# A routed mixture-of-experts start rewritten: token rows by ScalarE and GpSimd, nine weight pieces split ahead of the gather

## The chip, the cores and the metric

The kernel runs on one core of a Trainium2 chip. The time is that of one execution in microseconds (us) on the device; lower is better. The core's engines are TensorE (PE, matmuls), VectorE (DVE), ScalarE (ACT), GpSimd (POOL) and SyncE (SP, which here only issues DMAs). Each engine works through its own instructions in order and waits on semaphores for the others.

## What is computed

Two transformer layers on 512 tokens of 1024 columns, then a state-space and pooling block. Layer 0 has dilated attention, layer 1 attention with forgetting; each is followed by a mixture of 16 experts, and only that part is touched here. Cut to it:

```python
def hierarchical_moe(h, wg_r, bg_r, we_r, be_r, w_gate, w_up, w_down):
    t = h.reshape(-1, d)                                  # 512 tokens
    g_prob = softmax(t @ wg_r + bg_r)                     # 4 groups of experts
    g_onehot = one_hot(argmax(g_prob)); g_w = max(g_prob)
    e_sel = einsum('nge,ng->ne', (t @ we_r + be_r).reshape(-1, 4, 4), g_onehot)
    top_v, top_i = top_k(e_sel, 2)                        # two experts of four
    gates = ...                                           # softmax(top_v) * g_w, zero elsewhere
    hid = silu(einsum('nd,edf->nef', t, w_gate)) * einsum('nd,edf->nef', t, w_up)
    y = einsum('nef,efd->nd', hid * gates[..., None], w_down)

hf = rmsnorm(x, norm_ffn[i]) * (1 + sc_f) + sh_f
x = x + g_f * hierarchical_moe(hf, ...)
```

## The kernel before

**Routing.** `moe_route` goes over four tiles of 128 tokens (t = 0 to 3), right behind the mixer's out-projection. For each it scales the rows, transposes them for PE (L850), multiplies by the router weights (L853), computes the inverse norm `tn_r`, forms the logits `lg` (L1205), and `route_tile` (L874 to L891) picks group and experts with short DVE instructions; `route_rank` (L899, L900) counts each token's place in its expert's list. L1209 forms the normed and shifted row `hn` in one DVE instruction of 128x1024, which writes the columns in another order (k major), so that a later transpose meets contiguous columns; SP writes it to `hd` in HBM (L1210).

**Lists and gathers.** In `moe`, `listed(e)` compares ranks with places (`oh`, L948), multiplies by the token numbers on PE (L952), writes the list `tidx` (L953, DVE) and has POOL gather up to 96 rows of `hd` into `xg` (L966). Three `xg` buffers are cleared by POOL beforehand (L1241). `route_gates` (L919 to L941) computes the gates with DVE and two exponentials on ACT.

**Overflow.** If an expert has over 96 tokens, a branch (`tc.If`, L1084) does the rest. Here it has none; still every engine reads the flag, branches, and passes a skip block in which it waits for its own instructions and, on SP and POOL, for the DMAs of its queues. Work that is behind the branch on one engine and waits for another engine's work behind the branch waits for that engine to have passed it.

**Weights.** An expert has six pieces of 0.5 MB: c = 0 to 3 hold gate and up, c = 4 and 5 down. `expert_loads` has SP issue them in order into raw buffers: `est` (7 of them, `DL['nes']`), `esp` (2, for c = 5), and four `x` buffers. The first nine steps of it (`n0` = 8, and one each for the later tiles) are issued in the routing. Matmuls are done in fp32r with the operand split in a high and a low half, three products for one: `split_weights` has ACT write the high half (L316) and DVE the low half (L317) into one of nine `ehl` buffers, used in turn, and the raw buffer is then free for the next load. The first expert is taken plain, in fp32 and without a split: transposed rows in `xTf` (L1021), matmuls on the raw pieces. Piece c = 5 is plain for every expert.

**Order.** PE's instructions are in the order of the code (`manual_schedule`); those of the other engines are placed by a scheduler that interleaves what is independent. `load(n)` stands for n steps of: split a piece, issue the next load.

**Experts.** `step(e)` runs gate and up of expert e (L154), between them the transposes of the next expert's rows (L1019 for the plain form, L487 for the split one), then the hidden part and the down product of the expert before, and `listed(e + 3)`.

## Time and profile before

| | us |
|---|---|
| runs | 1825.73, 1826.6, 1831.0 |
| median | 1826.6 |
| the profiled execution, its own time | 1824.57 |
| its span (first to last instruction) | 1822.6 |
| PE busy in the span | 1624.6 (89%) |
| DVE, ACT, POOL busy | 1285.6, 919.7, 123.9 |
| mixture of layer 0, from the first gather to the last issue of an expert piece | 734 to 904 |
| the same of layer 1 | 1279 to 1448 |

A row of the timeline gives the start, the duration, the engine, the line, the operation, what it writes and reads, and in brackets how long the engine stood idle ahead of it and what ended that. "DVEq L1084" stands for the sequencer of DVE at the branch, SPq for an issue by SP. In the table of stretches PEclk is the granted clock of PE as a share of the full 2.4 GHz, and DMA is the mean busy share of the 16 DMA engines.

### The profile page before, as it was taken

The numbers are of one execution on the slowest core, as the hardware profiler recorded it, in microseconds if no ns is written. First come the engines' busy times: TensorE is split into PE (matmuls) and PEld (weight loads), VectorE is DVE, ScalarE is ACT, GpSimd is POOL, SyncE is SP. The second block draws the span as 40 slices with busy tenths as digits, with TensorE's granted clock in tenths as the row PEclk, the third lists the DMA queues.
The fourth block names the chain that finished last, engine by engine and source line by source line (L and its number), as shares of the span: only waits on it lengthen the run. The fifth ranks groups of instructions, "written<-read, shape, count | busy, mean of one in ns | idle before, by whom it ended". The sixth has DMA issues, their size and how long they took to land. (4 is left out here: it accounts for less than half of the span.)

```text
span 1822.6 us, 29089 instructions
## 1 busy us (share of the span) xinstructions
PE 1624.6 (89%) x10222; PEld 1381.7 (76%) x10223; DVE 1285.6 (71%) x3181; ACT 919.7 (50%) x1975; POOL 123.9 (7%) x101
## 2 busy tenths in 40 slices
PE   5979999999999998699859999898689959999998
PEld 3778999989989987456548798887455647788886
DVE  6758677677776656688755768757688746998564
ACT  4536455565555652566533655642556534353443
POOL 1000000000000000133210000000132210000000
PEclk9999999999999998799989999999799979999999
DMA  8786546466564235799872231226799854233331
GB/s 291 225 282 206 170 146 195 148 180 187 153 182 120 84 100 193 235 306 323 271 185 71 71 89 51 76 82 208 232 315 314 266 168 116 78 106 99 111 117 72
DMA packets 263995, 310.90 MB, mean 171 GB/s; under 512 B 33887, under 2 KB 177867, under 8 KB 263836
## 3 DMA queue, kind: packets, MB, share of 16 engines
q1 hardware_dynamic: 255708, 291.89, 51.1%
q0 software_dynamic: 8128, 17.02, 4.2%
q8 instruction: 84, 1.38, 0.3%
q14 instruction: 75, 0.61, 0.1%
HBM read 287.88 MB, written 38.90 MB: 179 GB/s over the span
## 5 line engine op out<-in xcount | busy, mean ns | idle before, releaser
L154 PE MATMUL mm<-whi,hThi 128*128 128x384 f32 (+2 forms) x1128 | 401.7, 356 | 5.4 <-DVE vlo L420 2.5
L154 PE MATMUL mm<-whi,hTlo 128*128 128x384 f32 (+2 forms) x1128 | 382.4, 339 | 0.8 <-DVE hTlo L741 0.6
L154 PE MATMUL mm<-wlo,hThi 128*128 128x384 f32 (+2 forms) x1128 | 381.1, 338 | 0.0
L317 DVE TENSOR_TENSOR wlo<-wst,whi 128x768 fp32r<-128x768 f32 (+2 forms) x200 | 199.6, 1009 | 69.4 <-ACT whi L316 66.9
L154 PEld LDWEIGHTS mm<-whi,hThi 128*128 128x128 f32 x1128 | 214.2, 190 | 15.0 <-DVE vlo L420 3.1
L316 ACT ACTIVATE whi<-wst 128x768 fp32r<-128x768 f32 (+2 forms) x200 | 176.1, 890 | 92.7 <-PE mm L154 54.3
L317 DVE TENSOR_TENSOR ehl<-est,ehl 128x1024 fp32r<-128x1024 f32 x144 | 175.7, 1220 | 61.5 <-ACT ehl L316 47.2
L154 PEld LDWEIGHTS mm<-whi,hTlo 128*128 128x128 f32 x1128 | 213.9, 190 | 4.4 <-DVE hTlo L741 1.8
L154 PEld LDWEIGHTS mm<-wlo,hThi 128*128 128x128 f32 x1128 | 214.8, 190 | 1.9 <-issue 0.6
L316 ACT ACTIVATE ehl<-est 128x1024 fp32r<-128x1024 f32 x144 | 152.1, 1058 | 110.5 <-DMA est<-in_w_up_dram 44.1
L249 DVE SCALAR_TENSOR_TENSOR adacc<-ast,csil,adacc 128x512 f32<-128x512 f32 x168 | 125.9, 750 | 66.0 <-DMA ast<-in_w_ada_dram 64.2
L154 PE MATMUL mm<-ehl,xTh 128*96 128x512 f32 x480 | 153.3, 400 | 0.0
L154 PE MATMUL mm<-hThi,whi 128*128 128x512 f32 (+1 forms) x288 | 107.1, 372 | 0.7 <-ACT sza L1925 0.6
L154 PE MATMUL mm<-hTlo,whi 128*128 128x512 f32 (+1 forms) x288 | 105.9, 368 | 0.5 <-DVE hTlo L311 0.3
L154 PE MATMUL mm<-hThi,wlo 128*128 128x512 f32 (+1 forms) x288 | 105.7, 367 | 0.0
L416 ACT ACTIVATE raw<-mm 128x256 f32<-128x256 f32 x126 | 47.9, 380 | 108.4 <-PE mm L154 108.0
L421 DVE TENSOR_REDUCE qss<-sq 128x4 f32<-128x256 f32 x128 | 52.9, 413 | 61.6 <-ACT sq L418 61.4
L154 PE MATMUL mm<-ehl,xTl 128*96 128x512 f32 x240 | 94.8, 395 | 0.0
L154 PEld LDWEIGHTS mm<-ehl,xTh 128*96 128x96 f32 x480 | 73.2, 162 | 25.8
L489 DVE TENSOR_TENSOR pTl<-tp,pTh 128x512 fp32r<-128x512 f32 (+1 forms) x112 | 68.4, 628 | 23.3 <-ACT pTh L488 22.6
L154 PE MATMUL av<-pTh,vhi 128*64 128x128 f32 x400 | 77.7, 230 | 0.4 <-ACT pTh L488 0.4
L487 PE MATMUL tp<-cst,pexp 128*128 128x128 f32 x400 | 64.2, 279 | 15.4 <-DVE pTl L489 11.7
(474 smaller groups left out, 3393.0 us busy)
## 6 DMA issues: line engine op xcount, KB each, us to landing
ast<-in_w_ada_dram SPq DMA_DIRECT2D x192, 256.0 KB
wst<-in_a_w_in_dram SPq DMA_DIRECT2D x192, 192.0 KB
est<-in_w_gate_dram SPq DMA_DIRECT2D x124, 256.0 KB
est<-in_w_up_dram SPq DMA_DIRECT2D x124, 256.0 KB
wst<-in_w_in_dram SPq DMA_DIRECT2D x32, 512.0 KB
est<-in_w_down_dram SPq DMA_DIRECT2D x30, 512.0 KB
esp<-in_w_down_dram SPq DMA_DIRECT2D x30, 512.0 KB
wst<-in_b_w_in_dram SPq DMA_DIRECT2D x64, 192.0 KB
```

Source lines behind the costliest of these rows:

```text
L154: self.nc.tensor.matmul(out, lhsT=l, rhs=r, start=n_first and i == 0, stop=n_last and i == nt - 1)
L249: last = nc.vector.scalar_tensor_tensor(acc, st, self.csil[:, k:k + 1], acc, op0=ALU.mult, op1=ALU.add)
L316: nc.scalar.activation(hi, st, AF.Copy)
L317: nc.vector.tensor_sub(lo, st, hi.bitcast(F32))
L416: nc.scalar.activation(raw[:, t].rearrange("p a b -> p (a b)"), p[:, :256], AF.Copy)
L421: nc.vector.tensor_reduce(ss[:, 4 * t:4 * t + 4], sq.rearrange("p (g d) -> p g d", d=HD), axis=AX.X, op=ALU.add)
L487: nc.tensor.transpose(p[:, j * q:(j + 1) * q], blocks[c + j], self.ident[:q, :q])
L489: self.mark = nc.vector.tensor_sub(lo[:, :m * q], p[:, :m * q], hi[:, :m * q].bitcast(F32))
```

## The change

1. The raw buffers `est` are eight instead of seven, and `n0` is nine instead of eight.
2. The shift row `rh` is written in the k-major order when it is made (`row(..., by=KC)`), by a strided ACT copy instead of a plain one, twice a layer.
3. L1209 goes. ACT writes `hn` with a scaled copy that reads with a stride (L1202 of the changed kernel), and POOL adds the shift row (L1203).
4. The first nine pieces are split ahead: the high halves on ACT (L1015), the low halves (L1016) of the first four on POOL, ahead of the first gather in the code, of the next two on POOL behind the second gather, of the others on DVE, behind the branch (one of the nine is the plain c = 5 piece, so eight are split). A load follows each low half.
5. The first expert is split like the others; the plain form is gone.
6. The gates are issued behind the second list's `tidx` (`issue_after`).
7. The overflow branch's skip block now lies straight behind the branch (`preferred_fallthrough_block=False`), its body behind it.

```diff
-DL['n0']=8
-DL['nes']=7
+DL['n0']=9
+DL['nes']=8
...
-    def row(self, pool, col, tag, bufs=1):
+    def row(self, pool, col, tag, bufs=1, by=1):
...
-            nc.scalar.activation(out[:, h * 512:(h + 1) * 512], p, AF.Copy)
+            n = 512 // by
+            nc.scalar.activation(out.rearrange("p (k q) -> p q k", k=by)[:, h * n:(h + 1) * n], p.rearrange("p (q k) -> p q k", k=by), AF.Copy)
...
-        nc.vector.tensor_scalar(idx, p[:q, 0:1], p[:q, 1:2], 4096.0, op0=ALU.add, op1=ALU.add)
+        self.idx_ins = nc.vector.tensor_scalar(idx, p[:q, 0:1], p[:q, 1:2], 4096.0, op0=ALU.add, op1=ALU.add).ins
...
-    def expert_split(self):
+    def expert_split(self, low=None):
...
-            if len(w) == 5 or w is self.W[0]:
+            if len(w) == 5:
...
-            self.split_weights(hl[:, 0], hl[:, 1], st)
+            if low is None:
+                self.split_weights(hl[:, 0], hl[:, 1], st)
+            else:
+                self.nc.scalar.activation(hl[:, 0], st, AF.Copy)
+                low.append(lambda ve: ve.tensor_sub(hl[:, 1], st, hl[:, 0].bitcast(F32)))
...
-            if len(w[k]) == 1:
-                terms = [(x[k], w[k][0])]
-            else:
-                wh, wl = w[k]
-                terms = [(x[0][k], wh), (x[0][k], wl), (x[1][k], wh)]
+            wh, wl = w[k]
+            terms = [(x[0][k], wh), (x[0][k], wl), (x[1][k], wh)]
...
-        with tc.If(any_rv > 0):
+        with tc.If(any_rv > 0, preferred_fallthrough_block=False):
...
-        return (self.mod_row("rs", self.scale_cols(l, 4, ("nf", l))), self.mod_row("rh", self.mod_part(l, 3)),
+        return (self.mod_row("rs", self.scale_cols(l, 4, ("nf", l))), self.mod_row("rh", self.mod_part(l, 3), by=KC),
...
-                by = lambda x: x.rearrange("p (q k) -> p k q", k=KC)
-                nc.vector.scalar_tensor_tensor(ho.rearrange("p (k q) -> p k q", k=KC), by(h), r, by(shrow), op0=ALU.mult, op1=ALU.add)
+                nc.scalar.activation(ho.rearrange("p (k q) -> p k q", k=KC), h.rearrange("p (q k) -> p k q", k=KC), AF.Copy, scale=r)
+                nc.gpsimd.tensor_add(ho, ho, shrow)
...
+            low = []
+            for _ in range(9):
+                self.expert_split(low)
+            low = [low[:4], low[4:6], low[6:]]
+
+            def lows(i, ve):
+                for f in low[i]:
+                    f(ve)
+                    next(self.loads, None)
+
+            lows(0, nc.gpsimd)
             ohs = [listed(0)]
             self.route_counts(self.rt, R)
             ohs.append(listed(1))
-            self.route_gates(self.rt, R["lg"], R)
+            lows(1, nc.gpsimd)
+            with self.tc.issue_after(self.idx_ins):
+                self.route_gates(self.rt, R["lg"], R)
             self.overflow(pm, R, hd, l)
-            load(4)
             with self.tc.manual_schedule(engines={mybir.EngineType.PE}):
-                xs[0] = self.expert_in(pm, xgs[0], True)
-            load(2)
+                xs[0] = self.expert_in(pm, xgs[0])
+            lows(2, nc.vector)
             listed(2, True)
-            load(self.NHL - 6)
```

ACT in layer 0, from the gates' exponentials to the branch, before; `est` and `x` are raw pieces, `ehl` split ones:

```order
L920 ACTIVATE rt_ge_8961<-rt_ge_8961 128x16
L925 ACTIVATE rt_ex_8966<-rt_ex_8966 128x4
L316 ACTIVATE ehl_9476<-est_8485 128x1024
L316 ACTIVATE ehl_9482<-est_8488 128x1024
L316 ACTIVATE ehl_9488<-x_1753_8621 128x1024
L316 ACTIVATE ehl_9558<-x_1782_8757 128x1024
L316 ACTIVATE ehl_9564<-x_1811_8894 128x1024
L316 ACTIVATE ehl_9571<-est_9432 128x1024
L1083 TENSOR_LOAD rt_anyi_8946
L1084 COMPARE_AND_BRANCH
```

and the same place in the changed kernel, up to the branch, then from behind the skip block to the first expert's transposed rows:

```order
L1202 ACTIVATE hn_8896<-hn_8769,tn_r_8773 128x1024
L921 ACTIVATE rt_ge_9006<-rt_ge_9006 128x16
L926 ACTIVATE rt_ex_9011<-rt_ex_9011 128x4
L1015 ACTIVATE ehl_8935<-est_8470 128x1024
L1015 ACTIVATE ehl_8937<-est_8473 128x1024
L1077 TENSOR_LOAD rt_anyi_8984
L1078 COMPARE_AND_BRANCH
...
L1015 ACT_TABLE_LOAD
L1015 ACTIVATE ehl_8939<-est_8476 128x1024
L1015 ACTIVATE ehl_8941<-est_8479 128x1024
L1015 ACTIVATE ehl_8949<-est_8492 128x1024
L489 ACTIVATE xTh_9479<-tp_9481 128x384
```

The last high half ahead of the branch in before read a piece that SP issued only after a low half had freed its buffer; now two high halves stand ahead of the branch and six behind it (three of the six, of the same form, are left out between the second and the last), all of pieces issued in the routing, and the first `xTh` follows them.

POOL in layer 0, before:

```order
L1241 MEMSET xg_1818_8924 96x1024
L966 DMA xg_1816_8920<-hd_1648_8235,tidx_8926 96x1024
L966 DMA xg_1817_8922<-hd_1648_8235,tidx_8926 96x1024
L1083 TENSOR_LOAD rt_anyi_8946
L1084 COMPARE_AND_BRANCH
```

and in the changed kernel, up to the branch and from behind the skip block on:

```order
L1203 TENSOR_TENSOR hn_8896<-hn_8896,rh_8206 128x1024
L967 DMA xg_1817_8927<-hd_1648_8235,tidx_8933 96x1024
L1016 TENSOR_TENSOR ehl_8935<-est_8470,ehl_8935 128x1024
L1077 TENSOR_LOAD rt_anyi_8984
L1078 COMPARE_AND_BRANCH
...
L1016 TENSOR_TENSOR ehl_8937<-est_8473,ehl_8937 128x1024
L1016 TENSOR_TENSOR ehl_8939<-est_8476,ehl_8939 128x1024
L1016 TENSOR_TENSOR ehl_8941<-est_8479,ehl_8941 128x1024
L967 DMA xg_1818_8929<-hd_1648_8235,tidx_8933 96x1024
L1016 TENSOR_TENSOR ehl_8943<-est_8482,ehl_8943 128x1024
L1016 TENSOR_TENSOR ehl_8945<-est_8486,ehl_8945 128x1024
```

The second gather moved from straight behind the first to behind the branch and three low halves; the skip block on POOL waits for the first gather to land. In layer 1 two low halves stand ahead of the branch and two ahead of the second gather.

## Rows read from the trace of the kernel before

**Rows 1.** The table of stretches; columns: stretch, length, busy us per engine, clock, DMA, GB/s.

```profile
740.00:745.00 5.00, 1.51 (x8) 1.25 (x8) 1.55 (x2) 1.60 (x2) 0.00 (x0) 0.50 0.45 154
...
750.00:755.00 5.00, 5.00 (x19) 2.33 (x18) 2.64 (x5) 2.59 (x5) 0.00 (x0) 0.99 0.93 268
...
770.00:800.00 30.00, 30.00 (x149) 19.98 (x148) 28.08 (x42) 20.06 (x30) 10.80 (x7) 1.00 1.00 315
...
880.00:900.00 20.00, 16.22 (x70) 10.35 (x69) 14.14 (x21) 10.62 (x17) 6.77 (x3) 0.83 0.99 318
```

**Rows 2.** Waits of PE, 728 to 760 us: total, times, longest.

```profile
PE tp L1019 <- DVEq L1084: 7.5, 1, 7.5
...
PE tp L952 <- ACT xTf L1021: 3.8, 1, 3.8
```

**Rows 3.** Timeline of DVE; start, us, what, and the idle time ahead.

```profile
725.88 0.24 DVE L1205 SCALAR_TENSOR_TENSOR lg<-av,tn_r,rbias 128x20 f32<-128x20 f32 x1
726.03 2.04 DVE L1209 SCALAR_TENSOR_TENSOR hn<-hn,tn_r,rh 128x1024 f32<-128x1024 f32 x1
...
732.79 0.22 DVE L953 TENSOR_SCALAR tidx<-tp 96x1 int32<-96x1 f32 x1
...
739.64 1.21 DVE L317 TENSOR_TENSOR ehl<-x,ehl 128x1024 fp32r<-128x1024 f32 x1
```

**Rows 4.** Timeline of PE, first and second expert of layer 0.

```profile
741.01 1.51 PE L1019 MATMUL tp<-cst,xg 96*128 96x96 f32 x8 [7.55 <-DVEq L1084]
...
746.63 2.00 PE L154 MATMUL mm<-est,xTf 128*96 128x512 f32 x2
...
752.21 0.83 PE L487 MATMUL tp<-cst,xg 96*128 96x96 f32 x8
752.87 3.60 PE L154 MATMUL mm<-est,xTf 128*96 128x512 f32 x8
...
758.02 0.68 PE L154 MATMUL mm<-ehl,xTh 128*96 128x512 f32 x2
...
764.29 0.30 PE L952 MATMUL tp<-rt_tg,oh 128*96 128x5 bf16 x4
```

**Rows 5.** Timeline of ACT.

```profile
730.69 1.99 ACT L316 ACTIVATE ehl<-est 128x1024 fp32r<-128x1024 f32 x2
...
743.21 1.06 ACT L316 ACTIVATE ehl<-est 128x1024 fp32r<-128x1024 f32 x1 [7.70 <-DMA est<-in_w_up_dram]
744.45 1.28 ACT L1021 ACT_TABLE_LOAD   x1 [0.18 <-ACTq L1084]
745.75 0.49 ACT L1021 ACTIVATE xTf<-tp 128x384 f32<-128x384 f32 x1
```

**Rows 6.** Timeline of SP's issues, then of POOL.

```profile
728.10 0.33 SPq L1210 DMA_DIRECT2D hd<-hn  x1
...
745.55 0.34 SPq L995 DMA_DIRECT2D est<-in_w_gate_dram  x1
...
757.29 0.39 SPq L998 DMA_DIRECT2D est<-in_w_down_dram  x1
762.06 0.33 SPq L995 DMA_DIRECT2D est<-in_w_gate_dram  x1
...
733.87 1.03 POOL L966 DMA_INDIRECT xg<-hd,tidx  x1 [13.98 <-DVE rt_o L934]
```

**Rows 7.** Timeline of PE in layer 1.

```profile
1291.90 2.00 PE L154 MATMUL mm<-est,xTf 128*96 128x512 f32 x2
```

**Rows 8.** A group of POOL (busy, mean ns); three lines' durations (min/median/max ns).

```profile
L1241 POOL MEMSET xg<- 96x1024 f32 x6 | 5.5, 955 | 191.8 <-PE sc L154 191.8
...
L620 ACT ACTIVATE UR<-av x16: 1075/1092/1109, 156.8 to 667.1; 64x512 f32<-64x512 f32 x16
...
L564 ACT ACTIVATE UN<-av x16: 575/589/590, 97.5 to 628.9; 64x512 f32<-64x512 f32 x16
...
L1209 DVE SCALAR_TENSOR_TENSOR hn<-hn,tn_r,rh x8: 2041/2273/2320, 693.9 to 1271.0; 128x1024 f32<-128x1024 f32 x8
```

More of the change, by code (lines that the diff above doesn't have):

```diff
@@ L1009, in expert_split, with expert_in @@
             hl = self.t(self.wp, [P, 2] + list(st.shape[1:]), F32R, "ehl", self.NHL)
-            self.split_weights(hl[:, 0], hl[:, 1], st)
-            w.append(list(zip(pick(hl[:, 0]), pick(hl[:, 1]))))
-    def expert_in(self, pool, xg, plain=False):
-        if plain:
-            f = self.t(pool, [P, KC, self.CAP], F32, "xTf", 1)
-            for c in range(0, KC, 4):
-                p = self.tp()
-                for k in range(4):
-                    self.nc.tensor.transpose(p[:, k * self.CAP:(k + 1) * self.CAP], xg[:, (c + k) * P:(c + k + 1) * P],
-                                             self.ident[:self.CAP, :self.CAP])
-                self.nc.scalar.activation(f[:, c:c + 4].rearrange("p a b -> p (a b)"), p[:, :4 * self.CAP], AF.Copy)
-            return [f[:, k] for k in range(KC)]
+            if low is None:
[3 more added lines that the diff above has]
+                low.append(lambda ve: ve.tensor_sub(hl[:, 1], st, hl[:, 0].bitcast(F32)))
+            w.append(list(zip(pick(hl[:, 0]), pick(hl[:, 1]))))
+    def expert_in(self, pool, xg):
         return self.transpose_split(pool, [xg[:, k * P:(k + 1) * P] for k in range(KC)], KC, "xT", self.CAP)
@@ L1152, in overflow, with mod_row @@
                             self.scatter(R["xd"], idx, y)
-    def mod_row(self, tag, col, bufs=1):
-        return self.row(self.rp, col, tag, bufs)
+    def mod_row(self, tag, col, bufs=1, by=1):
+        return self.row(self.rp, col, tag, bufs, by)
     def moe_rows(self, l):
-        return (self.mod_row("rs", self.scale_cols(l, 4, ("nf", l))), self.mod_row("rh", self.mod_part(l, 3)),
+        return (self.mod_row("rs", self.scale_cols(l, 4, ("nf", l))), self.mod_row("rh", self.mod_part(l, 3), by=KC),
                 self.mod_row("rg", self.mod_part(l, 5), 2))
```

## The prediction, made before the changed kernel ran

> **What bounds the kernel now.** I first read the table of stretches [rows 1], which separates the stage that the change touches from what follows. In 740 to 745 us TensorE (PE) works 1.51 of 5 us at a granted clock of 0.50, the lower level of 1.2 GHz; from 750 the clock is at its upper level, 2.4 GHz. In 770 to 800 PE works all 30 us, with VectorE (DVE) at 28.08 and the DMA share at 1.00; in 880 to 900 PE has gaps and the DMA share is 0.99. So the first experts run at PE's pace and the last of layer 0 at the weight loads' pace. Time is won only if both the first expert and the stream of loads start earlier.
>
> Then the waits of PE [rows 2]: the two largest ahead of the first expert are 7.55 us for DVE to pass the overflow branch and 3.8 us for ScalarE (ACT) to write xTf. The rows of DVE [rows 3] show the chain behind the first: lg at 725.88, then L1209 for 2.04 us, the routing list only behind its end at 728.07, the first tidx at 732.79, five low halves up to 740.85; PE's transposes of xg0 start 0.16 us after [rows 4]. The rows of ACT [rows 5] show the second: its sixth high half waits 7.70 us for a piece of weights that SP issued shortly ahead of the branch, then a table load and xTf. The first expert's first matmul is at 746.63 [rows 4]. SP's issues [rows 6]: the first behind the branch at 745.55, a dense run up to 757.29, then a pause until 762.06 for want of free buffers. Layer 1 has the same picture 545 us later, first matmul at 1291.90 [rows 7]. I reckon with one layer and double it.
>
> **The change part by part.**
>
> 1. *L1209 leaves DVE.* The list chain begins behind lg at 726.12 instead of 728.07 [rows 3]: 1.9 us earlier, first tidx written at 731.1 instead of 733.01. At t = 0 to 2 the same 2.0 to 2.3 us [rows 8] lie beside the out-projection on PE: nothing there.
>
> 2. *hn by ACT and POOL.* ACT's scaled copy reads 128x1024 with a stride. Lower end: the plain split of that shape, 1.06 us [rows 5]. Upper end: L620 against L564, the same 512 columns, strided write against plain, 1092 against 589 ns [rows 8], so 1.06 x 1.85 = 1.97. I take 1.5. POOL's addition has no row of its kind. Lower end: POOL's memset of 1024 columns, one stream, 0.955 us [rows 8]; upper end: three such streams (two reads and a write) one behind the other, 2.87; I take two, 1.9, since the write can run beside the reads. So hd of the last tile is issued at 726.1 + 1.5 + 1.9 = 729.5 instead of 728.10. Gather 0 follows the hd issue by 5.77 us in before [rows 6]: 735.3 instead of 733.87, 1.4 later (bounds 0 to 2.9). On ACT that copy stands ahead of the gates' exponentials, which wait for DVE anyway.
>
> The Trainium skill, "GPSIMD Engine Reference", section 3.1, measures an fp32 addition of 2048 columns at 4497 ns on this engine; half of it as an estimate, 2.25 us, would move gather 0 by 0.35 us more and leave the sum as it is. No run here has shown it yet.
>
> 3. *Gates behind the second tidx.* They leave the list's way and still come before the branch, done near 735. ACT's exponentials, and the two high halves queued behind them, then start near 732.5. Price: nothing, as PE doesn't need the gates before the first expert ends.
>
> 4. *Nine pieces split ahead, no low half on DVE before the branch.* DVE passes the branch near 735 instead of 741. ACT: two high halves to 734.9 (1.99 for two [rows 5]), branch and table load 1.5 (0.18 + 1.28 [rows 5]) to 736.4, six more high halves at 0.99 each to 742.4, then the first xTh, 0.5, at 742.9; first matmul near **743.2** instead of 746.63, a gain of 3.4. ACT no longer waits for a late piece: all nine were issued long before the branch. The transposes of xg0 need its landing: at the earliest 1.03 us behind the issue, at the latest 7.1 (741.01 - 733.87, when PE read it in before [rows 4, 6]), so 736.3 to 742.4, middle 739.4; with 1.51 us of transposes they end by 743.9 at the worst, which would put the first matmul at 744.6.
>
> 5. *Four low halves on POOL for the first expert, two more behind gather 1.* POOL runs gather 0 (1.03), the first low half (to 738.2), then its branch, whose skip block waits until xg0 has landed (739.4). Three low halves at 1.9: 741.3, 743.2, 745.1. Gather 1 at 745.1 instead of 735.21, ten us later; landed 746.2 to 752.2. Before transposed xg1 at 752.21 [rows 4], so that delay is hidden, with no slack at the worst end. Two more low halves: 748.5 and 750.4, needed when the second expert starts, near 754.
>
> 6. *First expert in three terms.* Sixteen plain matmuls become 24; the second expert's 24 take 764.29 - 758.02 less 0.6 for the transposes in between, 5.7 us at the full clock [rows 4], against 8 plain ones in 3.60 us, 7.2 for 16. If the clock rises as long behind the first matmul as in before (3.5 us), the gate and up half ends at about 752.5; if it rises at the same time as before, at 753.7; before at 756.47 [rows 4]. A lead of 2.8 to 4.0 us, middle **3.4**.
>
> 7. *Loads.* SP's first issue behind the branch waits for POOL's first low half: about 738.3 instead of 745.55. One piece fewer (14 for 15) was issued before. The next three follow POOL's low halves (741.3, 743.2, 745.1), so near 750 some 20 to 21 pieces are out where before had 17 to 18. At 318 GB/s [rows 1] a piece of 0.524 MB is 1.65 us, so that lead is worth about 5 us; but before's pause ahead of 762.06 [rows 6] shows that the buffers are full by then, and what survives is the lead of PE (3.4), which frees them, plus one more raw buffer (up to 1.65), less the split buffers that the first expert now holds (its down piece until after the second expert's first half). I take 3.3.
>
> 8. *What ACT and DVE get instead.* After the branch ACT has five more high halves, DVE three to five more low halves of 1.21 us [rows 3]. In 750 to 755 they were busy 2.59 and 2.64 of 5 us; in 770 to 800 DVE is at 28.08 of 30 [rows 1], so what is left over by 770 would press there. Upper price 2 us per layer; I take none. The strided row copies (two a layer) cost ACT at most 0.5 us each in the mixer's stage: none on the path.
>
> Sum: 3.3 us a layer, 6.6 for two. The profiled execution has a span of 1822.6 and took 1824.57, 2.0 below the median 1826.6; subtracting from the median gives **1820.0 us**, 0.36%. A measurement of this kernel tells about 0.3%, 5.5 us, from no change.
>
> **The rivals.**
>
> *A. The DVE chain waits for POOL.* If an addition on POOL holds up DVE instructions with two SBUF operands, the list chain, full of such (L883, L890, L948), waits until POOL's last hn addition ends near 729.5, later than 728.07. Then the list isn't earlier, the first matmul falls to about 745, and the two low halves that DVE runs after the branch stretch by one POOL instruction each. Gain 1 to 1.5 a layer: 1824. For it: the addition stands beside just that chain. Against it: no two such instructions overlap in before, so no row decides. The Trainium skill, "SBUF — State Buffer", section "Who interferes with whom", says just this: a DVE instruction with two SBUF inputs and a GpSimd instruction that reads SBUF block each other for a whole instruction, whoever is first. No run here shows it yet. Chance 0.17.
>
> *B. The loads keep the old pace.* The last of layer 0 waits for loads (0.99 [rows 1]); if the split buffers held by the first expert and SP's order behind POOL eat the lead, the start is earlier and the end isn't: 0.5 to 1 us a layer, 1825. For it: the pause ahead of 762.06. Against it: one buffer more. Chance 0.18.
>
> *C. Slower: POOL paces the start.* With s for a POOL addition, the second expert's first low half ends near 736.3 + s + 3s + 1.3 + 2s = 737.6 + 6s (for s up to 3; beyond, the first low half is later than xg0 and it goes with 8s). It is level with before's 758.02 at s = 3.4 and later above that; SP's issues hang on the same low halves. At s = 4 (three streams and a stall behind DVE) the second expert starts 4 to 5 us late in each layer: 1835. Against it: the upper end of the rows is 2.87. Chance 0.13.
>
> *D. More.* If the whole lead in loads stays (5 us) and PE starts 1 us earlier still, since t = 3 no longer queues behind L1209 on DVE: 5.5 a layer, 1815.5. Chance 0.10.
>
> **How the numbers follow.** The forecast has 0.42, its own range 2 to 5 us a layer, 1816.5 to 1822.5; of it 0.36 lies below 1821.1. Faster by over 0.3%: 0.36 + 0.10 = 0.46. Within 0.3%: 0.06 + 0.17 + 0.18 = 0.41. Slower: 0.13. The range leaves out the far part of C and the best of D: 1812 to 1829.
>
> **What would show it.** Right: the first tidx near 731 and 1.9 us ahead of before's; no L1209 on DVE; POOL's additions at 1.9 to 2.3 us; ACT without a wait of over 2 us between branch and xTh; first matmul at 742.5 to 744.6; SP's first issue behind the branch near 738. A: list instructions of over 1.5 us, or tidx not earlier. B: first matmul early, last loads of layer 0 at the same time as before. C: POOL additions over 3.4 us, PE waiting for a low half or for xg1. The prediction is wrong if PE's first matmul isn't earlier, or if its lead is gone by the end of the experts.

## The result, and the profile after

The changed kernel takes 1838.3 us (median of 20 runs, 1832.17 to 1843.09) against 1826.67 of the kernel before (20 runs, same chip): a ratio of **1.0066, 95% interval 1.0054 to 1.0077**. That is slower by 12 us, or 0.66%. I had forecast 1820.0 in a range of 1812 to 1829, with 0.13 for slower. The profiled execution took 1836.61 us with a span of 1834.9 (before 1822.6).

Busy times of the changed kernel, from the page; and its chain of work that ended last, by engine:

```profile
PE 1626.7 (89%) x10242; PEld 1388.5 (76%) x10243; DVE 1310.9 (71%) x3177; ACT 946.2 (52%) x1993; POOL 171.1 (9%) x121
...
PE 18%; DMA 7%; DVE 3%; ACT 1%; issue 1%; POOL 0%; SPq 0%; DVEq 0%; ACTq 0%; POOLq 0%
```

PE does 2 us more than before, DVE 25.3 more, though DVE lost the eight L1209 (17.8 us) and two low halves net (150 before, 148 now, 2.4 us). The split of the first expert adds it six short instructions (2.5 us). The others have become longer, by some 43 us in all. In the chain DMA stands at 7%; before it was 4%.

The same four stretches as in [rows 1], with the same columns:

```profile
740.00:745.00 5.00, 1.51 (x8) 1.25 (x8) 2.15 (x7) 4.99 (x6) 2.58 (x2) 0.50 0.34 101
750.00:755.00 5.00, 2.37 (x16) 1.84 (x16) 4.96 (x6) 0.00 (x0) 4.82 (x3) 0.50 0.61 179
770.00:800.00 30.00, 30.00 (x149) 19.96 (x148) 28.95 (x44) 21.01 (x33) 10.62 (x6) 1.00 0.97 296
880.00:900.00 20.00, 17.88 (x88) 11.42 (x87) 14.77 (x24) 10.87 (x17) 5.35 (x4) 1.00 0.98 308
```

In 750 to 755 PE works 2.37 of 5 us at a granted clock of 0.50, the 1.2 GHz level, where it worked all 5 at 0.99 before. DMA has fallen from 0.93 to 0.61. DVE and POOL are both "busy" all the time (4.96 and 4.82), and the next rows show what that is: DVE in layer 0, then POOL.

```profile
731.35 2.01 DVE L878 SCALAR_TENSOR_TENSOR rte<-rtes,rt_v,desc 128x4 f32<-128x4 f32 x1
...
738.20 2.49 DVE L935 TENSOR_TENSOR rt_o<-rt_o,rt_o 128x16 f32<-128x16 f32 x1
...
745.54 6.57 DVE L1016 TENSOR_TENSOR ehl<-est,ehl 128x1024 fp32r<-128x1024 f32 x2 [3.19 <-ACT ehl L1015]
...
753.28 4.86 DVE L949 TENSOR_TENSOR oh<-cst,rt_rk 128x384 bf16<-128x384 f32 x1
```

```profile
731.00 2.34 POOL L1203 TENSOR_TENSOR hn<-hn,rh 128x1024 f32<-128x1024 f32 x1 [2.53 <-ACT hn L1202]
737.24 1.03 POOL L967 DMA_INDIRECT xg<-hd,tidx  x1 [3.90 <-DVE oh L949]
738.29 2.36 POOL L1016 TENSOR_TENSOR ehl<-est,ehl 128x1024 fp32r<-128x1024 f32 x1
743.06 7.96 POOL L1016 TENSOR_TENSOR ehl<-est,ehl 128x1024 fp32r<-128x1024 f32 x3 [2.42 <-ACT ehl L1015]
751.17 1.80 POOL L967 DMA_INDIRECT xg<-hd,tidx  x1 [0.15 <-POOL ehl L1016]
753.01 4.70 POOL L1016 TENSOR_TENSOR ehl<-est,ehl 128x1024 fp32r<-128x1024 f32 x2
```

Each long DVE row overlaps a POOL addition and ends behind it. L878 (four columns, 0.22 us elsewhere in the list) takes 2.01 beside the addition to hn; L935 (16 columns, 0.16 before) takes 2.49 beside the first low half and ends at 740.69, 0.04 behind it; L949 (0.55 elsewhere) takes 4.86 and ends 0.43 behind the pair that ends at 757.71. Two low halves on DVE take 6.57, where [rows 3] has 1.21 each.

In layer 1 it is worse, since two low halves of POOL stand ahead of its branch and two behind it; DVE, then POOL:

```profile
1288.10 4.68 DVE L935 TENSOR_TENSOR rt_o<-rt_o,rt_o 128x16 f32<-128x16 f32 x1
1292.81 0.22 DVE L937 TENSOR_TENSOR rt_g<-rt_og,rt_o 128x64 f32<-128x64 f32 x1
1293.07 2.40 DVE L940 CAST rt_tg<-rt_g 128x64 bf16<-128x64 f32 x1
1295.50 2.23 DVE L942 TENSOR_TENSOR rt_g<-rt_g,rt_tg 128x64 f32<-128x64 f32 x1
...
1298.12 5.43 DVE L942 TENSOR_TENSOR rt_g<-rt_g,rt_tg 128x64 f32<-128x64 f32 x1
```

```profile
1288.08 4.65 POOL L1016 TENSOR_TENSOR ehl<-est,ehl 128x1024 fp32r<-128x1024 f32 x2
1293.00 4.65 POOL L1016 TENSOR_TENSOR ehl<-est,ehl 128x1024 fp32r<-128x1024 f32 x2 [0.27 <-issue]
...
1298.82 4.63 POOL L1016 TENSOR_TENSOR ehl<-est,ehl 128x1024 fp32r<-128x1024 f32 x2
```

Four instructions of the gates (the four over 2 us), 0.85 us together in the kernel before, take 14.74. L937 runs undisturbed in the gap between two POOL pairs. All of them stand ahead of the branch on DVE, and PE's first transposes wait for DVE to pass it. The largest waits of PE, layer 0 (two lines) and layer 1, beside [rows 2]:

```profile
PE tp L488 <- DVEq L1078: 6.6, 1, 6.6
...
PE tp L953 <- DVE xTl L490: 4.8, 2, 4.6
...
PE tp L488 <- DVEq L1078: 18.0, 1, 18.0
```

PE's timeline, layer 0 and the first matmul of layer 1, beside [rows 4, 7]:

```profile
742.96 1.51 PE L488 MATMUL tp<-cst,xg 96*128 96x96 f32 x8 [6.64 <-DVEq L1078]
746.88 1.17 PE L154 MATMUL mm<-ehl,xTh 128*96 128x512 f32 x2 [2.41 <-ACT xTh L489]
752.63 0.41 PE L953 MATMUL tp<-rt_tg,oh 128*96 128x5 bf16 x4 [4.58 <-DVE xTl L490]
...
761.54 0.40 PE L154 MATMUL mm<-ehl,xTl 128*96 128x512 f32 x1
...
1305.68 1.17 PE L154 MATMUL mm<-ehl,xTh 128*96 128x512 f32 x2
```

And SP's issues of layer 0, beside [rows 6]: the first is at 742.60, and then they follow POOL's low halves: 751.05 comes 0.03 us behind the third's end, and the next, 755.41, behind the first of the pair behind gather 1.

```profile
742.60 0.35 SPq L996 DMA_DIRECT2D est<-in_w_gate_dram  x1
...
745.46 0.33 SPq L996 DMA_DIRECT2D est<-in_w_gate_dram  x1
...
747.77 0.33 SPq L996 DMA_DIRECT2D est<-in_w_gate_dram  x1
...
751.05 0.33 SPq L999 DMA_DIRECT2D est<-in_w_down_dram  x1
755.41 0.33 SPq L996 DMA_DIRECT2D est<-in_w_gate_dram  x1
```

**Where the time is.** To compare executions I count from t0, the first transposes of normed rows in a layer's routing (before 685.74 and 1229.27, after 689.64 and 1235.32), to the start of the last scatter of the mixture. Layer 0 takes 243.5 us before and 245.2 after, layer 1 243.7 and 249.9. So of the 12.3 us between the two spans 1.7 lie in layer 0's mixture and 6.2 in layer 1's; 0.5 between and behind them; 3.9 lie ahead of layer 0's routing. Of these 3.9 us, 0.8 come with the two strided copies of the shift row (1.93 us together instead of 1.09); the other 3.1 lie ahead of everything that the change touches and belong to this one pair of executions. The ratio rests on 20 of each.

In layer 1 the chain of work that ended last (start, duration, what) runs from the gates on DVE over a low half of POOL to the piece that this low half lets SP issue:

```profile
1288.10 4.69 DVE rt_o L935
...
1298.82 2.36 POOL ehl L1016
1301.19 0.33 SPq L996
...
1301.57 4.51 DMA est<-in_w_up_dram
```

Of the 205 us from the lists of layer 1 on, landings of weights take 56% of this chain and PE 23%; before it was 27% and 46%.

### The profile page after: what moved, and what is told of

The parts are those of the page before. It is cut to its first block, busy times and chain, and to the rows that moved or that the text cites. A ratio compares the mean times of both kernels' runs of the same rounds, so it can differ in the third digit from the quotient of the medians.

```text
span 1834.9 us, 29197 instructions
## 1 busy us (share of the span) xinstructions
PE 1626.7 (89%) x10242; PEld 1388.5 (76%) x10243; DVE 1310.9 (71%) x3177; ACT 946.2 (52%) x1993; POOL 171.1 (9%) x121
## 5 line engine op out<-in xcount | busy, mean ns | idle before, releaser
L318 DVE TENSOR_TENSOR ehl<-est,ehl 128x1024 fp32r<-128x1024 f32 x138 | 167.5, 1219 | 45.7 <-ACT ehl L317 42.5
L317 ACT ACTIVATE ehl<-est 128x1024 fp32r<-128x1024 f32 x138 | 144.8, 1057 | 89.7 <-DMA est<-in_w_up_dram 46.8
L154 PE MATMUL mm<-ehl,xTh 128*96 128x512 f32 x512 | 169.9, 414 | 2.4 <-ACT xTh L489 2.4
L154 PEld LDWEIGHTS mm<-ehl,xTh 128*96 128x96 f32 x512 | 81.6, 169 | 31.8 <-ACT xTh L489 2.9
L154 PE MATMUL mm<-ehl,xTl 128*96 128x512 f32 x256 | 104.8, 409 | 0.0
L154 PE MATMUL av<-pTl,vhi 128*64 128x128 f32 x400 | 77.0, 228 | 2.3 <-DVE pTl L490 2.3
```

The source lines that it names most:

```text
L154: self.nc.tensor.matmul(out, lhsT=l, rhs=r, start=n_first and i == 0, stop=n_last and i == nt - 1)
L317: nc.scalar.activation(hi, st, AF.Copy)
L318: nc.vector.tensor_sub(lo, st, hi.bitcast(F32))
```

## The experiments

Each ratio is to the kernel before, run on the same chip, with its 95% interval. The theory after the first look: POOL's additions shut DVE out, and the delay reaches the end through PE's start or through the loads. The rival: the new work (hn on ACT, three products for the first expert, more splits ahead) costs by itself.

**e1 and e2: the two halves of the change.** e1 is the changed kernel with hn again by DVE and the plain row:

```diff
-nc.scalar.activation(ho..., h..., AF.Copy, scale=r)
-nc.gpsimd.tensor_add(ho, ho, shrow)
+nc.vector.scalar_tensor_tensor(ho..., by(h), r, by(shrow), op0=ALU.mult, op1=ALU.add)
```

> The changed kernel with the row hn made by DVE in one instruction again (and the shift row written plainly): only the early splits, the first expert in parts, the gates behind the second list and the branch's layout are left of the change. Theory 1 (a POOL addition that reads SBUF holds up DVE instructions until it ends): the low halves on POOL still stand beside DVE's gates and its own two low halves, so most of the loss stays: 5 to 11 us above before, DVE rows of over 2 us where 0.2 or 1.2 are usual, and PE's wait of some 18 us at the branch of layer 1 still there. Theory 2 (the loss comes from hn, its strided copies and its later hd): within 3 us of before.

Measured 1843.12 us, **1.0091 (1.0060 to 1.0123)**: some 17 us above before, more than the 5 to 11 that I had expected. e2 is the reverse: the kernel before with only hn by ACT and POOL and the k-major row.

```diff
-nc.vector.scalar_tensor_tensor(ho..., by(h), r, by(shrow), op0=ALU.mult, op1=ALU.add)
+nc.scalar.activation(ho..., h..., AF.Copy, scale=r)
+nc.gpsimd.tensor_add(ho, ho, shrow)
...
-self.mod_row("rh", self.mod_part(l, 3))
+self.mod_row("rh", self.mod_part(l, 3), by=KC)
```

> The kernel before with only the row hn made by ACT and POOL (and the shift row in the other order). Theory 1: one instruction of the routing list stretches to some 2.0 us in each tile while POOL adds, which takes the place of the DVE instruction of 2.04 us that is gone; the list is no earlier, hd is issued 3 us later: 0 to 5 us above before over both layers. Theory 2: 8 to 13 us above before, as the changed kernel is.

Measured 1826.83, **0.9996 (0.9975 to 1.0018)**. The hn part is neutral in time, though its first matmul comes 4.1 and 3.6 us earlier than before's (56.8 and 59.0 us behind t0); the loss is in the split ahead. e1 shows the shutting out at its plainest, DVE and then POOL:

```profile
740.61 9.55 DVE L1016 TENSOR_TENSOR ehl<-est,ehl 128x1024 fp32r<-128x1024 f32 x1 [1.80 <-ACT ehl L1015]
750.17 1.21 DVE L1016 TENSOR_TENSOR ehl<-est,ehl 128x1024 fp32r<-128x1024 f32 x1
```

```profile
739.82 9.26 POOL L1016 TENSOR_TENSOR ehl<-est,ehl 128x1024 fp32r<-128x1024 f32 x4
```

One low half on DVE takes 9.55 us, until four of POOL's in a row are over; the next takes 1.21. PE waits 21.8 us for DVE to pass the branch in layer 0, 21.5 in layer 1.

**e3 and e4: what on POOL does it.** The kernel before, with work that nobody needs on POOL behind the second gather: in e3 four additions that read the free xg buffer, in e4 memsets that take about as long (in layer 0 10.3 us, the additions 9.6).

```diff
 ohs.append(listed(1))
...
+for _ in range(4):
+    nc.gpsimd.tensor_add(jk, jk, jk)       # e4: nc.gpsimd.memset(jk[:, :n], 0.0), n = D, D, D // 2
 self.route_gates(self.rt, R["lg"], R)
```

> The kernel before, and on POOL behind the second gather four additions of 96x1024 whose result nobody waits for (zeros added to zeros in the third gather's buffer, some 2.35 us each, one of them ahead of the branch). Theory 1: DVE's low halves beside them (1.21 us) stretch to over 2.4 us, DVE passes the branch 2 to 7 us late, 1 to 8 us a run above e4. Theory 3 (POOL's long instructions cost only because other engines wait for their results or for their place in POOL's queue): no DVE instruction changes, same time as e4.

> The same place on POOL taken for the same time by memsets (two of 1024 columns and one of 512 for each addition), which write SBUF and read nothing. Theory 1 (it is the reading that shuts DVE out): DVE's low halves stay at 1.21 us, same time as before within 2 us. Theory 1b (any POOL instruction shuts DVE out): as e3. Theory 3: the same as e3, whatever that is.

Measured: e3 1830.37, 1.0016 (0.9989 to 1.0044); e4 1830.21, 1.0030 (1.0006 to 1.0055). In time they don't differ, where I had expected e3 to be 1 to 8 us slower; in the rows they do. e4 is 0.3% slower than before, just clear of noise, where I had expected no change, and why stays open. e3's POOL, then its DVE:

```profile
738.56 2.70 POOL L1282 TENSOR_TENSOR xg<-xg 96x1024 f32<-96x1024 f32 x1
745.16 6.89 POOL L1282 TENSOR_TENSOR xg<-xg 96x1024 f32<-96x1024 f32 x3 [3.90 <-DMA vrows<-in_pool_scale_dram]
```

```profile
739.43 1.91 DVE L941 TENSOR_TENSOR rt_g<-rt_g,rt_tg 128x64 f32<-128x64 f32 x1
...
745.61 2.52 DVE L317 TENSOR_TENSOR ehl<-est,ehl 128x1024 fp32r<-128x1024 f32 x1 [1.89 <-ACTq L1084]
...
748.32 1.97 DVE L948 TENSOR_TENSOR oh<-cst,rt_rk 128x384 bf16<-128x384 f32 x1
```

The same for e4:

```profile
748.27 6.71 POOL L1283 MEMSET xg<- 96x1024 f32 x8 [2.31 <-DMA vrows<-in_pool_scale_dram]
```

```profile
749.10 1.23 DVE L317 TENSOR_TENSOR ehl<-est,ehl 128x1024 fp32r<-128x1024 f32 x1 [3.20 <-ACTq L1084]
```

Beside additions DVE's instructions stretch to the end of the addition (a 0.22 us one to 1.91); beside memsets the low halves keep 1.22 to 1.23. POOL's reading shuts DVE out, its writing alone doesn't. PE's wait for DVE's branch grows from 7.5 to 9.3 and 10.9 us in e3 and stays 7.5 in e4. These 2 to 3 us don't reach the first matmul: in e3 the wait for xTf behind the branch shrinks from 3.8 to 2.2, and the first matmul stands 60.1 and 62.0 us behind t0, before 60.9 and 62.6. So e3 shows that DVE is shut out, but not what a late start of PE would cost.

**e5 and e6: all low halves on DVE.** The changed kernel with `lows(0, nc.vector)` and `lows(1, nc.vector)`; e6 also with hn by DVE, and with `lows(1)` written behind the branch, so that no addition is left on POOL. The scheduler puts all eight ahead of the branch in both.

```diff
-lows(0, nc.gpsimd)
+lows(0, nc.vector)
...
-lows(1, nc.gpsimd)
+lows(1, nc.vector)          # e6: not here, but ahead of lows(2, nc.vector)
```

> The changed kernel with all eight early low halves on DVE (they come to stand ahead of the branch); hn stays with ACT and POOL. Theory 1 (the loss is POOL's low halves shutting DVE out): no DVE low half over 1.3 us, PE's waits at the branch 7 to 10 us in both layers instead of 6.6 and 18.0, time 1822 to 1831, that is within 0.3% of before. Theory 4 (the loss is in the other parts of the change: the first expert in parts, the gates behind the list, the branch's layout, the ninth piece): 1834 to 1842.

> As the kernel before it, and hn by DVE too: no addition on POOL at all, what is left of the change is the order, the ninth piece and the first expert in parts. Theory 1: within 4 us of before, 1823 to 1832; the list begins 2.0 us later than in the kernel before it. Theory 4: 1834 to 1842.

Measured: e5 1824.53, **1.0020 (0.9999 to 1.0041)**; e6 1826.3, **1.0042 (1.0022 to 1.0062)**. e5 is as expected, within 0.3% of before: it gets back most of the loss with a longer wait of PE than the changed kernel has in layer 0 (12.6 us for DVE's branch, in layer 1 13.8). e6 is some 8 us above before where I had expected at most 4; its layer 0 has a stall of its own (PE waits 20.1 us for xg0), told at the end.

**e7 and e8: POOL's low halves kept, but made shorter or put behind.** e7 cuts each of POOL's low halves into four of 256 columns, so that DVE can come in between; e8 moves the six behind the branch and both gathers.

```diff
-low.append(lambda ve: ve.tensor_sub(hl[:, 1], st, hl[:, 0].bitcast(F32)))
+for q in range(4): ve.tensor_sub(lo[:, c], s[:, c], hi[:, c].bitcast(F32))   # e7, c the q-th 256 columns
...
-lows(0, nc.gpsimd)          # e8: here ahead of listed(0), lows(1, nc.gpsimd) behind listed(1)
 ...
 lows(2, nc.vector)
+lows(0, nc.gpsimd)          # e8
+lows(1, nc.gpsimd)
```

> The changed kernel with each low half on POOL cut into four instructions of 256 columns (some 0.6 us each). Theory 1a (DVE is shut out for the instruction that runs, and comes in at its end): DVE's small instructions wait at most 0.7 us, its low halves end within 2 us, the loss shrinks by half or more: 1827 to 1834. Theory 1c (as long as POOL has the next addition ready, DVE doesn't come in at all): DVE rows as long as a whole series of POOL's, 3 us and more, and 1835 to 1842.

> The changed kernel with both gathers ahead of the branch as in before, and all six POOL low halves behind it. Theory 1: DVE's gates run undisturbed (0.2 us each) and it passes the branch at about the same time in both layers, PE's wait of 18 us in layer 1 goes; DVE's two low halves behind the branch still stand until POOL is through (6 us and more), and with them xTl, for which PE waits 4 to 10 us a layer: 1829 to 1838. Theory 5 (what costs is the second gather, ten us later): 1822 to 1828.

Measured: e7 1834.38, **1.0074 (1.0046 to 1.0101)**; e8 1834.04, **1.0086 (1.0059 to 1.0112)**. Neither is better than the change. The ranges that I had expected were reckoned from a before of 1826.67, and before ran at 1820.8 on the chip of these two: e7 is some 13 us above it where theory 1a had at most 7, e8 some 16 where theory 1 had 2 to 11. In e7 DVE does come in (two low halves in 2.89 us), but POOL's 15 quarters take 15.59 and gather 1 comes at 753.65, so PE waits 9.6 us for xg1. In e8 the gates are undisturbed, and the two engines take turns, POOL then DVE:

```profile
740.39 18.21 POOL L1016 TENSOR_TENSOR ehl<-est,ehl 128x1024 fp32r<-128x1024 f32 x6 [5.23 <-ACT ehl L1015]
```

```profile
750.17 9.51 DVE L318 TENSOR_TENSOR ehl<-x,ehl 128x1024 fp32r<-128x1024 f32 x3
```

A POOL low half costs 3.03 us, a DVE one 3.17 instead of 1.21. PE's wait of 18 us is gone and the first matmul isn't late (59.6 us behind t0 in layer 0, 61.5 in layer 1; before 60.9 and 62.6), yet the kernel is as slow as the others with low halves on POOL. PE loses its time behind the first matmul: as theory 1 has it, it waits 7.7 and 8.1 us a layer for xTl, which stands behind DVE's low halves, and ACT begins the second expert's `sg` (its gate and up are done then) 88.5 us behind t0 instead of 78.8, in layer 1 92.0 instead of 80.9.

**e9, e10, e11: the best of both, tried.** e9 has no addition on POOL and four low halves on DVE ahead of the branch, the other four held behind the first xTl; e10 is the same with hn by ACT and POOL; e11 is e8 with DVE's two low halves held behind the first xTl.

```diff
-lows(0, nc.gpsimd)
+lows(0, nc.vector)
...
-lows(1, nc.gpsimd)
...
-lows(2, nc.vector)
+with self.tc.issue_after(self.mark.ins):   # mark: the first xTl
+    lows(1, nc.vector); lows(2, nc.vector); load(1)
```

> No addition on POOL at all: hn by DVE, the early low halves by DVE, four of them ahead of the branch and the other four (and the first of the later loads) held behind the first xTl, where e6 had all of them ahead of the branch. Theory 1 (what e5 and e6 still lost is PE's wait for eight or nine low halves ahead of the branch): PE's wait there falls from 12.6 to 20 us to 6 to 9, first matmul 3 to 5 us earlier than in e6 relative to the first gather, 1812 to 1822. Theory 4 (the first expert in parts or the ninth piece costs): as e6, 0.3 to 0.6% above before.

> The same with hn by ACT and POOL as in the change. Theory 1: DVE shut out once per tile for some 2 us, which takes the place of its own instruction of 2.04 us; within 3 us of e9.

> e8 with DVE's own two early low halves held behind the first xTl: six POOL low halves behind the branch, both gathers ahead. Theory 1 (DVE's low halves, shut out by POOL, hold up xTl in e8): PE's wait for xTl of 4 us goes, 3 to 6 us below e8 over both layers, still 0.2 to 0.6% above before, since the second gather's place is no longer the limit but POOL's low halves of 3 us each are. Theory 5 (POOL's own pace): as e8.

Measured: e9 1825.81, **0.9996 (0.9982 to 1.0011)**; e10 1825.26, **1.0003 (0.9988 to 1.0018)**; e11 1841.71, **1.0082 (1.0064 to 1.0100)**. Without low halves on POOL the split ahead is level with the kernel before, no better; I had expected e9 at 1812 to 1822, but in its layer 0 PE waits 15.7 us for xg0 (told at the end). e11 was expected below e8 and isn't: PE's waits for xTl go, but then it waits 4.5 and 2.5 us for the gates of the lists (L956), which in layer 0 now stand behind the low halves on DVE. The wait has moved; the order of xTl and DVE's low halves isn't what costs.

**e12 and e13: PE's start against the loads.** Both are the kernel before. e12 holds its splits, and the loads with them, behind the first expert's rows and the lists, so that DVE passes the branch early:

```diff
...
-load(4)
 xs[0] = self.expert_in(pm, xgs[0], True)
-load(2)
 listed(2, True)
-load(self.NHL - 6)
+with self.tc.issue_after(self.idx_ins):    # the last tidx written
+    load(self.NHL)
```

e13 leaves the start alone and holds SP: behind the branch three chained DMAs of one column each, the first of which reads xTf, stand ahead of the next piece.

```diff
...
+nc.sync.dma_start(jk[:, 0:1], xs[0][KC - 1][:, 0:1])
+for i in range(2):
+    last = nc.sync.dma_start(jk[:, i + 1:i + 2], jk[:, i:i + 1])
+with self.tc.issue_after(last.ins):
...
     next(self.loads, None)              # the third piece and all later ones
```

> The kernel before with nothing changed but the place of the first low halves: held on DVE behind the second listed expert's tidx, that is behind the branch. If PE's 7.5 us wait at the branch is for those five low halves alone, it falls to 3 to 6 us (then the landing of xg0 decides), the first matmul comes 1 to 4 us earlier a layer, and the time is 1 to 6 us below before; if the landing of xg0 decides anyway, no change.

> The kernel before, with SP's issues behind the branch held: ahead of them SP issues three tiny chained DMAs, the first of which reads the last column of xTf, so that the first piece behind the branch goes out some 6 to 9 us later than before's (59.8 us behind the start of the routing). The pieces of the first two experts are out by then, and the first matmul isn't touched by more than 1 us. Theory (the mixture goes at the pace of the loads): each mixture ends 4 to 8 us later, so 9 to 16 us in all, ratio 1.005 to 1.009. Rival (the start of the first expert on TensorE sets the end, loads have slack): within 2 us, ratio up to 1.001.

Measured: e12 1828.05, **1.0018 (1.0001 to 1.0035)**, with the first matmul 8.2 and 6.7 us earlier than before, more than expected, and no gain where I had expected 1 to 6 us. e13 1836.43, **1.0056 (1.0031 to 1.0081)**, with the first matmul 1.4 and 1.0 us earlier than before. SP in layer 0 of e13:

```profile
748.15 0.54 SPq L1286 DMA_DIRECT2D jk<-xTf  x1
749.91 2.53 SPq L1288 DMA_DIRECT2D jk<-jk  x2
752.53 0.55 SPq L995 DMA_DIRECT2D est<-in_w_gate_dram  x1
```

SP's first piece goes out 64.0 us behind t0 instead of 59.8, in layer 1 68.5 instead of 61.8: 4.2 and 6.7 later. The total rises by 10 us (5.7 to 14.8 by the interval), by about as much as the pieces were held. So an earlier first matmul by 7 to 8 us gains nothing, and a later issue of 4 to 7 us a layer costs half of it or more. Why e12 gains nothing can be read in its second expert: ACT begins that `sg` 78.1 and 81.5 us behind t0, before 78.8 and 80.9. The lead is spent by then: the loads are held with the low halves, so in layer 0 the piece of ACT's sixth high half is there only 62.7 us behind t0 (before 57.5), and the first expert's `sg` stands behind that high half and two more on ACT; PE waits 3.5 us for what follows from it (`hid`; before 1.3). So e12 says that an early first matmul is worth nothing while pieces come late, not that a lead kept through the experts would be worth nothing. In e13's one profiled execution the two mixtures end 2.6 and 1.9 us later from t0, less than the medians say; the profiled execution is the quickest of its runs (1830.86).

**e14: the change without what POOL adds.** The changed kernel with POOL's six low halves a layer left out; PE multiplies by the high half in their place.

```diff
+if len(low) < 6:
+    low.append(lambda ve: None)
+    w.append(list(zip(pick(hl[:, 0]), pick(hl[:, 0]))))
+    return
 low.append(lambda ve: ve.tensor_sub(hl[:, 1], st, hl[:, 0].bitcast(F32)))
```

> The changed kernel with the six low halves of POOL left out: TensorE multiplies the high half in their place, so the number of products is the same and the output is not the reference's. A raw buffer is free as soon as the high half is written and its other readers are done. Theory (POOL's low halves are the whole loss): the two waits for DVE to pass the branch shrink to under 2 us in both layers, the pieces go out earlier than in before, and the time is 1815 to 1824, ratio 0.994 to 0.999. Rival (what else the change does costs by itself: high halves of nine pieces on ACT, three products for the first expert, the held split buffers): 1830 or more, ratio over 1.002.

Measured 1823.01, **0.9976 (0.9960 to 0.9993)**: 4.4 us under the kernel before, and 0.9% under the changed one. So POOL's low halves are the whole loss, and all else in the change together would gain 0.24%, if its low halves cost nothing. PE's wait ahead of the first transposes is then

```profile
PE tp L488 <- DMA xg<-hd,tidx: 6.6, 1, 6.6
```

in layer 0, and 7.1 in layer 1: xg lands 5.7 us behind the issue of its gather (738.80 to 744.47). I had expected waits under 2 us and had left out that PE then still waits for this landing.

The runs side by side; all times from t0, layer 0 / layer 1. "Pieces" are the 0.5 MB pieces that SP has issued from just ahead of t0 to t0 + 100 us.

| | ratio | first matmul | pieces | last scatter |
|---|---|---|---|---|
| before | 1 | 60.9 / 62.6 | 33.0 / 31.5 | 243.5 / 243.7 |
| changed | 1.0066 | 57.2 / 70.4 | 32.5 / 27.0 | 245.2 / 249.9 |
| e1 | 1.0091 | 70.0 / 72.1 | 28.5 / 27.0 | 252.1 / 249.9 |
| e8 | 1.0086 | 59.6 / 61.5 | 29.5 / 27.0 | 250.8 / 247.5 |
| e9 | 0.9996 | 64.1 / 59.0 | 30.5 / 33.5 | 246.0 / 237.1 |
| e12 | 1.0018 | 52.7 / 56.0 | 33.5 / 30.5 | 240.2 / 249.0 |
| e13 | 1.0056 | 59.5 / 61.6 | 29.5 / 29.0 | 246.1 / 245.6 |
| e14 | 0.9976 | 59.6 / 61.6 | 33.0 / 31.5 | 242.4 / 240.9 |

Where SP has issued 27 to 29.5 pieces, the mixture ends 2 to 9 us later than before's, whether the first matmul was early or late; where it has issued 31.5 or more, it ends within 2 us of before's or earlier. The runs not shown lie the same way: e5 and e11 in layer 1, e6 in layer 0 and e7 in both have 27 to 29.5 pieces and end 2 to 8 us later; e2, e4 and e5 in layer 0 and e10 in both have 31.5 or more and end no later. From 30 to 31 pieces it goes either way, from 2.6 us earlier (e6, layer 1) to 5.3 later (e12, layer 1).

This column isn't a cause by itself. SP can issue only as buffers come free, and later on that hangs on PE's progress, so a PE held up by DVE also lowers the count. Only e13 moves the issues alone. In the changed kernel's layer 1 and in e1 the first matmul is late too (by 7.7 to 9.5 us), and in e8 the second expert is; in these runs what the loss owes to PE's waits for DVE and what to the loads isn't parted.

## Why the prediction was wrong, point by point

The step that failed is the price of nothing for DVE beside POOL's low halves (parts 3 to 6 of the prediction, and rival A with one list instruction and two low halves): e14 shows that these six low halves are worth the whole loss, 0.66% slower with them and 0.24% faster without. Part 7 then let a lead of 3.3 us a layer survive that was gone by the end of the first expert in layer 0, and was never there in layer 1.

**1, the list earlier: half right.** The first tidx comes 46.0 us behind t0 instead of 47.05, 1.05 earlier where I had 1.9. L878 stretched to 2.01 us beside the addition to hn took the rest: that is rival A, in the place where I had put it.

**2, hn by ACT and POOL: prices low, result near.** ACT's copy took 2.13 us (estimate 1.5, upper bound 1.97), POOL's addition 2.34 (estimate 1.9, within the bounds). The Trainium skill's "GPSIMD Engine Reference", section 3.1, from which I had put 2.25 beside it, was nearer. The issue of hd is 1.36 us later from t0, where I had 1.4. Gather 0 followed 0.5 earlier than before, not 1.4 later; it wasn't waiting for hd alone.

**3, the gates for nothing: the first step that failed.** I wrote "price: nothing, as PE doesn't need the gates before the first expert ends". PE doesn't need them, but they stand ahead of the branch on DVE, and PE waits for that branch. In layer 1 they cost 14.74 us instead of 0.85, and PE's wait for the branch is 18.0. Part 4 has DVE past the branch near 735, 49 us behind t0; PE's transposes, which wait for that, start 53.3 us behind t0 in layer 0 and 68.9 in layer 1.

**4, first matmul 3.4 us earlier: right in layer 0, not in layer 1.** 57.2 us behind t0 against 60.9, 3.7 earlier; ACT's eighth high half ends 56.8 behind t0, where the prediction has 56.7. In layer 1 it is 7.7 later. I had worked out one layer and doubled it; but the order is not the same in both, with one low half of POOL ahead of the branch in layer 0 and two in layer 1, as the section on the change says. That step was wrong in method.

**5, POOL's low halves: mis-sized.** 2.36 us alone, 2.65 in the three beside DVE, against 1.9. Gather 1 comes 61.5 us behind t0, 2.1 later than forecast; PE didn't wait for xg1.

**6, the first expert's end: failed.** Gate and up end at 761.94, 72.3 us behind t0; before 70.7. A lead of 3.4 became a lag of 1.6. The 4.58 us for xTl are most of the difference: xTl stands behind two low halves on DVE, which took 6.57 instead of 2.42, beside POOL's three. PE's granted clock stayed at 0.50 in 750 to 755, where it was 0.99 before.

**7, the loads: failed.** I let PE's lead (3.3 us a layer) survive to the end. In e12 a lead of 7 to 8 us at the first matmul was spent by the second expert, and in e2 one of 4 us brought nothing; so the first matmul is not the place to measure a lead. For the loads I had 20 to 21 pieces out where before had 17 to 18. SP did restart earlier (53.0 against 59.8 us behind t0), but then at POOL's pace, one piece for each low half; by t0 + 66 it was half a piece ahead of before in layer 0, and by t0 + 100 it had issued 0.5 fewer than before in layer 0 and 4.5 fewer in layer 1. At 1.65 us a piece [rows 1] that is 0.8 and 7.4 us; the mixtures end 1.7 and 6.2 later. e13 shows that held pieces alone give such a loss. What the loss would be with the loads on time and PE still waiting for DVE wasn't tried; e3 has the loads on time and DVE shut out, but PE starts on time in it.

**8, more work for ACT and DVE: right for the experts, not for the row copies.** DVE is busy 28.95 of 30 us in 770 to 800 with PE at 30.00, and e14, which has the same work there, is faster than before. The strided copies of the shift row, which I had put at nothing on the path, cost 0.8 us ahead of layer 0's routing, in e2 as in the changed kernel.

**The rivals.** A had the mechanism and a price far too small: one list instruction and two low halves, where the gates, the list of the third expert and xTl stood in the same way. The passage that I cited there, "SBUF — State Buffer", section "Who interferes with whom" of the Trainium skill, agrees with L935, L1016, e3 and e4 (a POOL instruction that only writes doesn't block). It speaks of a whole instruction; the rows show a DVE instruction kept out over two (4.68 us) and four (9.55 us) of POOL's in a row, which is what a price must reckon with. C had the sign and the wrong trigger: it decides from an addition of 3.4 us, but at 2.36 the kernel was already 12 us slower, since I had POOL's pace in it and not DVE's. B, the loads at their old pace, looked at one of the two places, and was too mild: the loads got slower.

## What to carry to other kernels

Before work goes to GpSimd, list every DVE instruction with two SBUF inputs that can be in flight beside it, and price each at worst at the rest of the whole run of back-to-back GpSimd instructions, however few columns it has (in e7 and e8 DVE came in between); then follow the smallest of them to whatever waits behind DVE, a branch above all. Where a stage is bound by weight loads, price a change by when the buffers come free and how many pieces are out at a given time, not by when the first matmul starts: in e12 that lead was spent by the second expert. And where two layers run the same code in another order, work out both.

## What was not expected of the hardware

- A CAST of 128x64 with one input, 0.25 us in the kernel before, took 2.40 us beside POOL's pair in the changed kernel and 1.94 in e3.
- Whether DVE gets a turn between two POOL additions varies: in e8 they alternate (3.03 us an addition), in e1 DVE gets none in four; in the changed kernel's layer 1 L935 gets none in a pair (4.68 us), and the CAST of 2.40 us comes in between the next two. No run tells what decides.
- It may go the other way round too. In layer 0 of e9 the gather on POOL, 1.03 us in [rows 6], took 5.93 us beside four low halves of DVE that began 0.4 us behind it, and in e6 11.85 beside nine:

```profile
734.12 5.93 POOL L967 DMA_INDIRECT xg<-hd,tidx  x1 [13.15 <-DVE rt_ge L920]
```

```profile
734.52 4.62 DVE L1016 TENSOR_TENSOR ehl<-est,ehl 128x1024 fp32r<-128x1024 f32 x4
```

The gather ends 0.9 us behind the last of the four, in e6 0.9 us behind the last of nine. In layer 0 of e5 and e10, where DVE's low halves begin 1.3 us behind the gather's end, it takes 1.37. But in layer 1 of e9 and e10 a gather that began 0.6 and 0.3 us behind the first of four low halves took only 1.57 and 1.74. So DVE's low halves don't hold up every gather, and no run was made to tell what does.
